# A hybrid retention and attention block on one core: `w_do` behind the first q,k gemm, both side products behind `w_o`, splits one gemm ahead, and a new order of the tail

## The chip, the cores and the metric

The kernel runs on one core of one Trainium2 chip. The metric is the time on the device in microseconds; the median of three runs of the kernel before is 1240.94 us (1239.77 to 1241.05).

## The reference

One layer on x of shape (1, 512, 1024), all in float32:

```python
u = rmsnorm(h, g_pre_mix)
proj = u @ w_in         # retention q,k,v,gate | dilated q,k,v | gates gr, ga
yr = rmsnorm(retention(rq, rk, rv, positions)) * silu(rg)      # 4 heads
ya_branch = yr @ w_ret_out
ya = dilated_attention(aq, ak, av, positions)   # 3 groups, merged by softmax denominators
yb_branch = ya @ w_dil_out
mixed = sigmoid(gr + b0) * ya_branch + sigmoid(ga + b1) * yb_branch
h = h + rmsnorm(mixed @ w_o, g_post_mix)
f = square(relu(rmsnorm(h, g_pre_mlp) @ w_up)) @ w_down
h = h + rmsnorm(f, g_post_mlp)
gate = sigmoid(rmsnorm(h, g_pre_ple) @ w_ple_gate + b_ple_gate)
h = h + rmsnorm(gate * (p @ w_ple_in), g_post_ple)
```

## The kernel before, in words

Every float32 product is made of three matmuls. `split` writes a float32 value as a rounded high part (ACT copies and rounds) and a low part (DVE subtracts); `PASSES` multiplies high with high, high with low and low with high. A gemm of 512 columns and 1024 rows of weights is 4 groups of 24 matmuls of 128x512, each in a PSUM bank; one of 512 rows is 4 groups of 12.

The order of the work is written out by hand. SP's queue carries the weight loads in one chain (`load`): a ring of raw 512 KB units, in the order of the list `loads`. `prep_next` splits the next unit of `plan` into a weight tile and tops up the ring; a gemm calls it while its last group runs. `later(lag, f)` puts off a piece by so many steps of PE, counted by `pump` after each group of three matmuls; `flush` runs all that is put off, and `drain` the steps of the attention that `filler` strews through gemms. What the text leaves free a scheduler decides: it orders each engine's queue, and pieces in `tc.high_priority()` come earlier.

The stages, with the names that the change touches:

1. `u`, transposed, then per dilated group g three gemms (v, q, k). `row_tables` makes the row of 1/rms (`rrow`) with four transposes on PE. The attention of a group runs inside the next gemms; `stream_order` moves its maxima and denominators between the two orders of tokens with small DMAs on ACT's and POOL's queues.
2. Four gate gemms; `gate_evac` applies the sigmoid and stores to DRAM (`zd`). Ahead of the fourth, `merge` combines the three groups: DVE scales them, 32 transposes on PE turn them round, and the result `y` goes to DRAM (`yd`). `left_sums` makes the sums of `u` for the 7-product scheme of `quartet`.
3. Four retention heads (`head`): a q,k gemm, rotation by `rope_pair`, then `quartet` with seven quarter products of two weight units each ("11", 1, "12", 2, 4, 7, "22"), scores, the retained products, and `flip`, which transposes the head's result and stores it (`yrd`).
4. `w_do`: two gemms of 48 on `yT` fetched from DRAM, times the fetched gate; `w_ro`: per head two gemms of 48 on `yrT`, fetched and split (`halved`) at the start of the head. `mix_out` joins both.
5. `w_o`: the first half with k outermost, then four token blocks; `wo_second` ends each block with its norm, and `residual_features` puts off the block's eight transposes (`to_features`) by a lag of 8. Then `e_first`, the first half of p @ w_ple_in, 24 matmuls, and `w_up`.
6. `w_up` and `w_down` by quartets, then the last two units of `w_down` by token block, again with `residual_features` and lag 8; the second half of p @ w_ple_in; then `w_ple_gate`, the first half by blocks, then the second, where `gated` makes sigmoid times e and `finish` the norm, the update and the two stores of a block. The last block is cut in two pieces of 256 columns.

The lag, for example, is given here:

```python
def residual_features(t, base, r, gain, rs, dst, rows, lag):
    ...
        later(lag, lambda v=v, n=n: to_features(dst, v, t, 4 * n))
```

## Time and profile before

| | |
|---|---|
| median of three runs | 1240.94 us |
| the profiled execution, its own time | 1239.94 us |
| its span | 1238.1 us |
| mean granted clock of PE in it | 0.996 |
| PE busy | 1213.0 us (98%), 5636 matmuls |
| DVE busy | 803.7 us (65%) |
| ACT busy | 593.1 us (48%) |
| POOL busy | 54.4 us (4%) |

The table is read from the first part of the profile's page. PE is busy nearly all the time, so what an edit can move lies in the stretches where PE waits, and in those where its granted clock is below full speed. The waits say for whom PE waited, the windows show how much of a stretch it was busy and how full the other engines were in it, and the timeline shows the single wait in its place. Weight loads into PE (PEld) overlap the matmuls. Ends of matmuls are modelled, so a row's length runs a little past the start of the next row.

### The profile page before, as it was taken

To read this page: it belongs to the slowest core of one execution; us is meant where nothing else is said; L and a number is where in the kernel's file an instruction comes from. 1 tells how busy PE (TensorE), PEld (TensorE's weight loads), DVE (VectorE), ACT (ScalarE), POOL (GpSimd) and SP (SyncE) were. 2 spreads that over 40 slices of the span, in tenths; PEclk is the share of its full clock that TensorE was granted. 3 is DMA by queue.
4 is the path that set the end of the run, shared out by engine and by line. 5 is a ranking of instruction groups with operands and counts; after the bars stand their busy time and mean duration, and the time that the engine had idled before them with its cause. 6 is when DMAs were issued, how large, how long until landed. Compare 5 with 4: busy or idle time off the path is not lost.

```text
span 1238.1 us, 15113 instructions
## 1 busy us (share of the span) xinstructions
PE 1213.0 (98%) x5636; PEld 990.2 (80%) x5636; DVE 803.7 (65%) x1215; ACT 593.1 (48%) x991; POOL 54.4 (4%) x100
## 2 busy tenths in 40 slices
...
GB/s 340 129 118 69 61 94 89 76 204 76 128 61 229 85 119 114 142 102 119 150 120 261 115 170 102 305 119 182 57 153 66 88 187 52 97 209 140 103 48 69
DMA packets 54617, 159.39 MB, mean 129 GB/s; under 512 B 8720, under 2 KB 8976, under 8 KB 54544
## 3 DMA queue, kind: packets, MB, share of 16 engines
...
q14 instruction: 29, 0.24, 0.1%
...
## 4 chain that ended last, share of the span: by engine, by line
PE 92%; DVE 3%; DMA 2%; ACT 2%; issue 1%; POOL 0%; DVEq 0%; POOLq 0%; ACTq 0%
PE a L233 50%; PE b L686 14%; PE a L999 11%; PE a L686 7%; PE b L464 2%; PE b L768 2%; PE b L494 2%; PE b L482 1%; DVE t L69 1%; ACT s L66 1%; PE b L753 1%; DMA t<-in_xT_dram 1%; DMA t<-in_x_dram 1%; DVE t L283 1%; PE b L306 1%
## 5 line engine op out<-in xcount | busy, mean ns | idle before, releaser
L69 DVE TENSOR_TENSOR w<-t,w 128x1024 fp32r<-128x1024 f32 (+1 forms) x248 | 296.1, 1204 | 158.2 <-ACT w L66 156.0
L66 ACT ACTIVATE w<-t 128x1024 fp32r<-128x1024 f32 (+1 forms) x248 | 257.5, 1045 | 280.0 <-PE a L233 100.8
L233 PE MATMUL a<-u,w 128*128 128x512 f32 x1536 | 376.5, 398 | 3.3 <-ACT u L66 2.4
L233 PEld LDWEIGHTS a<-u,w 128*128 128x128 f32 x1536 | 283.2, 189 | 66.8 <-issue 4.0
L69 DVE TENSOR_TENSOR t<-t,t 128x1024 f32<-128x1024 f32 (+4 forms) x193 | 194.4, 1031 | 23.5 <-ACT t L66 18.3
L686 PE MATMUL b<-w,t 128*128 128x512 f32 x696 | 162.5, 389 | 0.0
L686 PEld LDWEIGHTS b<-w,t 128*128 128x128 f32 x696 | 130.6, 188 | 27.1
L999 PE MATMUL a<-u,w 128*128 128x512 f32 x576 | 134.0, 389 | 0.0
L999 PEld LDWEIGHTS a<-u,w 128*128 128x128 f32 x576 | 108.1, 188 | 22.4
L233 PE MATMUL a<-w,u 128*128 128x512 f32 (+1 forms) x504 | 118.0, 390 | 5.1 <-ACT w L66 5.1
L233 PE MATMUL a<-t,w 128*128 128x512 f32 x480 | 110.5, 391 | 1.0 <-ACT t L66 0.6
L233 PEld LDWEIGHTS a<-w,u 128*128 128x128 f32 x504 | 91.7, 192 | 23.4 <-ACT w L66 5.1
L233 PEld LDWEIGHTS a<-t,w 128*128 128x128 f32 x480 | 89.8, 188 | 20.6 <-ACT t L66 1.3
L233 PE MATMUL a<-w,t 128*128 128x512 f32 x432 | 100.5, 391 | 0.0
L233 PEld LDWEIGHTS a<-w,t 128*128 128x128 f32 x432 | 80.6, 188 | 16.5
L69 DVE TENSOR_TENSOR t<-a,t 128x512 f32<-128x512 f32 x72 | 55.6, 773 | 58.2 <-ACT t L66 30.2
L66 ACT ACTIVATE s<-b 128x512 f32<-128x512 f32 (+1 forms) x74 | 44.6, 609 | 94.4 <-PE b L482 40.5
L468 DVE CUSTOM_DVE_ANT_0 s<-b,masks 128x128 f32<-128x128 f32 (+1 forms) x96 | 27.2, 321 | 84.7 <-PE b L464 84.7
L66 ACT ACTIVATE t<-t 128x512 fp32r<-128x512 f32 (+1 forms) x61 | 45.5, 770 | 38.3 <-DVE t L69 36.6
L66 ACT ACTIVATE s<-s,st 128x128 f32<-128x128 f32 (+1 forms) x96 | 40.0, 418 | 25.4 <-DVE st L471 25.3
L69 DVE TENSOR_TENSOR s<-a,t 128x512 f32<-128x512 f32 x40 | 26.4, 687 | 38.7 <-PE a L233 31.4
L66 ACT ACTIVATE t<-s 128x256 f32<-128x256 f32 (+3 forms) x90 | 39.1, 481 | 23.3 <-DVE s L69 19.7
...
## 6 DMA issues: line engine op xcount, KB each, us to landing
t<-in_w_in_dram SPq DMA_DIRECT2D x104, 512.0 KB
t<-in_w_down_dram SPq DMA_DIRECT2D x38, 512.0 KB
t<-in_w_up_dram SPq DMA_DIRECT2D x32, 512.0 KB
t<-in_w_ret_out_dram SPq DMA_DIRECT2D x16, 512.0 KB
t<-in_x_dram SPq DMA_DIRECT2D x8, 512.0 KB
...
```

Source lines behind the costliest of these rows:

```text
L66: nc.scalar.activation(o, i, f, **kw)
L69: nc.vector.tensor_tensor(o, x, y, op=op)
L233: nc.tensor.matmul(ps, l, r, start=(k == 0 and q == 0), stop=(k == n - 1 and q == 2))
L283: return nc.vector.scalar_tensor_tensor(o, x, s, y, op0=op0, op1=op1)
L306: nc.tensor.transpose(b[:, f * P:(f + 1) * P], src[:, f * P:(f + 1) * P], ident)
L464: nc.tensor.matmul(sb[hh][:, q * w:(q + 1) * w], at(qT, p0 + q)[rows, t * P:(t + 1) * P], at(kT, p0 + q)[rows, k0:k0 + w], start=True, sto ...
L468: nc.vector.tensor_tensor_reduce(out=sm[:, i, :], in0=sb[hh][:, q * w:(q + 1) * w], in1=mk, scale=1.0, scalar=NEG, op0=OP.add, op1=OP.max, ...
L482: nc.tensor.transpose(tb[:, c * P:(c + 1) * P], sm[:, i, j * P:(j + 1) * P], ident)
L494: nc.tensor.matmul(pv[:, s * HD:(s + 1) * HD], got["t"][:, c * P:(c + 1) * P], at(v, t - nb + 1 + j)[:, s * HD:(s + 1) * HD], start=(j == ...
L686: nc.tensor.matmul(ps[t], f(k, i, t), w[:, j, k2], start=(first and k == 0 and n == 0), stop=(k == 3 and n == 2), skip_group_check=not first)
L768: nc.tensor.matmul(b, sc[j][:, i1, c:c + P], vh[j][:, i2, :], start=(n == 0), stop=(n == last))
L999: nc.tensor.matmul(state["ps"][t], w[:, i, k2, t * P:(t + 1) * P], vT[:, x, k], start=(k == 0 and n == 0), stop=(k == 7 and n == 2))
```

## The change

- The gate columns come in the order 21 to 24; the first two gate gemms store to DRAM (`z0d`), the last two keep their result on chip (`z1`).
- The maxima and denominators of group 0 are put in stream order as soon as group 1 is started, and the eight scatters of `merge` that were on POOL's queue go to SP's.
- `merge` puts off its four turns (eight transposes each) by lags of 32 to 44, and splits each result at once into `yT`; `yd` goes.
- `w_do` and its weight units move from behind the last head to behind the q,k gemm of head 0, with `left_sums`; its product with `z1` goes to DRAM (`ybd`).
- `row_tables` is put off by 4 steps.
- In `w_ro` the operands of the next head are split between the two gemms of a head; `ybd` and `z0d` are fetched on POOL's queue.
- Both halves of p @ w_ple_in run behind `w_o`, both go to DRAM and are fetched on POOL's queue; the lags are 16 and 14 behind `w_o` and 12 behind `w_down`, and the `flush` ahead of `w_ple_gate` goes.
- In the tail the multiply with `g_post_ple` moves from `finish` to `gated`, and the updates of block 2 are issued behind the last block's first operations.

The diff, cut to its core:

```diff
-    for c in (23, 24, 21, 22):
+    for c in (21, 22, 23, 24):
         add_units(w_in, c)
     for h in range(H):
         add_units(w_in, 3 * h)
+        if not h:
+            for n in range(2):
+                add_units(w_do, n)
         add_quartet(lambda kh, nh, k, h=h: w_in[3 * h + 2 - nh, 2 * kh + k], EARLY)
-    for n in range(2):
-        add_units(w_do, n)
     for h in range(H):
         for n in range(2):
             add_units(w_ro[h], n)
     for n in range(2):
         add_units(a["w_o"], n)
-    add_units(a["w_ple_in"], 0)
+    for n in range(2):
+        add_units(a["w_ple_in"], n)
...
+        if g == 1:
+            stream_order(lambda c: sc[0][:, c], lambda t: M[0][:, t])
+            stream_order(lambda c: sc[1][:, c], lambda t: DEN[0][:, t])
...
-                eng = nc.gpsimd if c % 2 else nc.scalar
+                eng = nc.sync if c % 2 else nc.scalar
...
         def scaled(o, nt_, al):
...
-        for p in range(4):
+        def turn(p):
             b = bank()
             for c in range(4):
                 nc.tensor.transpose(b[:, c * P:(c + 1) * P], at(N[1], c)[:, p * P:(p + 1) * P], ident)
...
             for t in range(NT):
                 nc.tensor.transpose(b[:, t * P:(t + 1) * P], at(N[0], t)[:, p * P:(p + 1) * P], ident)
             tt(y, b, y, OP.add)
-            nc.scalar.dma_start(yd[p], y)
+            yh = big((P, 2, 512), F32R)
+            split(yh[:, 0], yh[:, 1], y)
+            yT.append(yh)
+
+        for p in range(4):
+            later(32 + 4 * p, lambda p=p: turn(p))
 
...
+        if not h:
+            flush()
+            left_sums()
+            for n in range(2):
+                gemm(2, list_feed(yT), do_out(n, z1[n]), wstat=True)
...
-    def gate_evac(n, k):
+    z0d = [pdr.tile([P, 512], F32, name=f"z0d{i}") for i in range(KT)]
+    ybd = [pdr.tile([P, 512], F32, name=f"ybd{i}") for i in range(KT)]
+
+    def gate_evac(n, k, keep=None):
         def f(t, ps):
-            z = half()
             i = 4 * n + t
-            tt(z, ps, rrow, OP.mult)
+            z = half() if keep is None else at(keep, t)
+            with tc.high_priority():
+                tt(z, ps, rrow, OP.mult)
             act(z, z, AF.Sigmoid, bias=cols[:, 1 + k, i:i + 1])
-            nc.scalar.dma_start(zd[k][i], z)
+            if keep is None:
+                nc.scalar.dma_start(z0d[i], z)
         return f
 
-    for n in range(4):
-        if n == 3:
+    def do_out(n, z):
+        def f(t, ps):
+            x = at(z, t)
+            tt(x, ps, x, OP.mult)
+            nc.scalar.dma_start(ybd[4 * n + t], x)
+        return f
+
+    for n in range(2):
+        gemm(4, uT, gate_evac(n, 0), wstat=True)
+    z1 = [pair_tiles() for _ in range(2)]
+    for n in range(2):
+        if n:
             drain()
             merge()
-            left_sums()
-        gemm(4, uT, gate_evac(n % 2, 1 - n // 2), wstat=True)
-
...
-    xs = fetch(yd)
-    yb = fetch(zd[1])
-    yT = halved(xs)
     xs = fetch(yrd[0])
-    for n in range(2):
-        gemm(2, list_feed(yT), do_out(n), wstat=True)
     yacc = [big((P, 2, 512)) for _ in range(4)]
+    yrT = halved(xs)
     for h in range(H):
-        yrT = halved(xs)
         if h + 1 < H:
             xs = fetch(yrd[h + 1])
         else:
-            z0 = fetch(zd[0])
-        for n in range(2):
-            gemm(2, list_feed(yrT), half_out(yacc, n, h == 0) if h + 1 < H else mix_out(n), wstat=True)
+            yb, z0 = ([at(x, i) for i in range(KT)] for x in (fetch(ybd, nc.gpsimd.dma_start), fetch(z0d, nc.gpsimd.dma_start)))
+        gemm(2, list_feed(yrT), half_out(yacc, 0, h == 0) if h + 1 < H else mix_out(0), wstat=True)
+        nxt = halved(xs) if h + 1 < H else None
+        gemm(2, list_feed(yrT), half_out(yacc, 1, h == 0) if h + 1 < H else mix_out(1), wstat=True)
+        yrT = nxt
 
...
-        residual_features(t, h1[t], r, g_pre, rs1[:, t:t + 1], vT, (r0[t], z), 8)
+        residual_features(t, h1[t], r, g_pre, rs1[:, t:t + 1], vT, (r0[t], z), 16 if t < 3 else 14)
         nc.gpsimd.dma_start(h1d[t], h1[t])
 
     gemm(4, mix, wo_second)
 
-    def e_first(t, ps):
-        x = half()
-        act(x, ps)
-        nc.scalar.dma_start(ed[t], x)
-
-    gemm(1, list_feed(pT), e_first)
+    def e_out(n):
+        def f(t, ps):
+            x = half()
+            act(x, ps)
+            nc.scalar.dma_start(ed[n][t], x)
+        return f
+
+    for n in range(2):
+        gemm(1, list_feed(pT), e_out(n))
     flush()
 
...
-        residual_features(t, h1[t], r, g_pre2, rs2[:, t:t + 1], hT, [part(t, n) for n in range(2)], 8)
-
-    pT = side()
-    e = {0: pair_tiles(), 1: pair_tiles()}
-    for t in range(NT):
-        nc.gpsimd.dma_start(at(e[0], t), ed[t])
-    gemm(1, list_feed(pT), lambda t, ps: act(at(e[1], t), ps))
-    flush()
+        residual_features(t, h1[t], r, g_pre2, rs2[:, t:t + 1], hT, [part(t, n) for n in range(2)], 12)
+
+    e = {n: pair_tiles() for n in range(2)}
+    for n in range(2):
+        for t in range(NT):
+            nc.gpsimd.dma_start(at(e[n], t), ed[n][t])
 
...
-        stt(z, ps, rs2[:, t:t + 1], b_ple[:, sl], OP.mult, OP.add)
+        i = stt(z, ps, rs2[:, t:t + 1], b_ple[:, sl], OP.mult, OP.add)
         act(z, z, AF.Sigmoid)
         x = at(e[n], t)[:, c]
-        tt(x, x, z, OP.mult)
-        parts.setdefault(t, []).append(sumsq(x))
-
-    def finish(t):
+        j = nc.vector.tensor_tensor(z, x, z, op=OP.mult)
+        parts.setdefault(t, []).append(sumsq(z))
+        tt(x, z, g_post3[:, sl], OP.mult)
+        return i.ins, j.ins
+
+    def finish(t, behind=None):
         r = rstd(parts[t], D)
         for n, sl in enumerate(halves):
-            tt(at(e[n], t), at(e[n], t), g_post3[:, sl], OP.mult)
-        for n, sl in enumerate(halves):
-            stt(h1[t][:, sl], at(e[n], t), r, h1[t][:, sl], OP.mult, OP.add)
+            with ExitStack() as st:
+                if behind:
+                    st.enter_context(tc.issue_after(behind[n]))
+                stt(h1[t][:, sl], at(e[n], t), r, h1[t][:, sl], OP.mult, OP.add)
             (nc.scalar if n else nc.sync).dma_start(out[t * P:(t + 1) * P, sl], h1[t][:, sl])
 
...
-                gated(t, 1, cs, ps[:, :w])
-        finish(t)
+                ins = gated(t, 1, cs, ps[:, :w])
+        if t != NT - 2:
+            if t == NT - 1:
+                finish(t - 1, ins)
+            finish(t)
```

Three places show how instructions move. Names are those of the tiles (w a weight tile, a and b banks of PSUM, t and s tiles in SBUF); `a<-w,t` is a matmul or an operation that writes a.

PE between `w_o` and `w_up`: in the kernel before, the end of the transposes of block 1, the side product (banks a_6723 to a_6753), the transposes of block 3 and the first matmuls of `w_up` (a_6788).

```order
L306 MATMUL b_6687<-ident,s_6621 128x128 x4
L233 MATMUL a_6723<-w_6434,t_6285 128x512 x3
L233 MATMUL a_6723<-w_6434,t_6288 128x512 x3
L233 MATMUL a_6733<-w_6434,t_6285 128x512 x3
L233 MATMUL a_6733<-w_6434,t_6288 128x512 x3
L233 MATMUL a_6743<-w_6434,t_6285 128x512 x3
L233 MATMUL a_6743<-w_6434,t_6288 128x512 x3
L233 MATMUL a_6753<-w_6434,t_6285 128x512 x3
L233 MATMUL a_6753<-w_6434,t_6288 128x512 x3
L306 MATMUL b_6765<-ident,s_6706 128x128 x4
L306 MATMUL b_6772<-ident,s_6709 128x128 x4
L233 MATMUL a_6788<-u_6444,w_6642 128x512 x6
```

In the changed kernel, from the end of the first side product:

```order
L234 MATMUL a_6725<-w_6420,t_6267 128x512 x3
L234 MATMUL a_6725<-w_6420,t_6270 128x512 x3
L307 MATMUL b_6737<-ident,s_6590 128x128 x4
L307 MATMUL b_6744<-ident,s_6593 128x128 x4
L307 MATMUL b_6781<-ident,s_6678 128x128 x4
L307 MATMUL b_6788<-ident,s_6681 128x128 x4
L234 MATMUL a_6754<-w_6614,t_6267 128x512 x3
L234 MATMUL a_6754<-w_6614,t_6270 128x512 x3
L234 MATMUL a_6764<-w_6614,t_6267 128x512 x3
L234 MATMUL a_6764<-w_6614,t_6270 128x512 x3
```

The transposes of blocks 2 and 3 stand together ahead of the second side product, whose banks begin with a_6754; `w_up` follows that product.

DVE at the start of head 0, where it prepares the second quarter's two weight units: in the kernel before w_3251 and w_3263, made between sums of weights and products of the rotation.

```order
L69 TENSOR_TENSOR t_3204<-s_3195,t_3204 128x512
L69 TENSOR_TENSOR w_3239<-t_3111,w_3239 128x1024
L69 TENSOR_TENSOR t_3111<-t_3111,t_3133 128x1024
L69 TENSOR_TENSOR w_3251<-t_3100,w_3251 128x1024
L69 TENSOR_TENSOR s_3280<-a_3232,t_673 128x512
L69 TENSOR_TENSOR w_3263<-t_3111,w_3263 128x1024
L69 TENSOR_TENSOR w_3274<-t_3242,w_3274 128x1024
```

In the changed kernel w_3409 is the second unit of that quarter; ahead of it stand products of `w_do` (banks a_3371 to a_3401) and sums of `left_sums` (t_3245, t_3249 and the low parts t_3256, t_3258).

```order
L69 TENSOR_TENSOR t_2637<-a_3371,t_2637 128x512
L69 TENSOR_TENSOR t_3258<-t_3245,t_3257 128x512
L69 TENSOR_TENSOR t_3256<-t_3249,t_3255 128x512
L69 TENSOR_TENSOR t_2638<-a_3386,t_2638 128x512
L69 TENSOR_TENSOR t_3249<-t_3249 128x2x256
L69 TENSOR_TENSOR t_3197<-t_3197,t_3219 128x1024
L69 TENSOR_TENSOR t_2638<-a_3401,t_2638 128x512
L69 TENSOR_TENSOR t_3258<-t_3249,t_3257 128x512
L69 TENSOR_TENSOR w_3409<-t_3197,w_3409 128x1024
```

The unit is made behind all of `w_do`'s products with z1, while before nothing of `w_do` or `left_sums` stood there.

DVE at the end of the program: before, block 2's updates (t_8946) ahead of the last piece's evacuation (s_9652), and the multiply with g_post_ple (t_9324) between the last sum and the norm.

```order
L283 SCALAR_TENSOR_TENSOR t_8946<-t_9264,st_9587,t_8946 128x512
L283 SCALAR_TENSOR_TENSOR t_8946<-t_9266,st_9587,t_8946 128x512
L283 SCALAR_TENSOR_TENSOR s_9652<-a_9627,rs_8943,t_9322 128x256
L69 TENSOR_TENSOR t_9266<-t_9266,s_9652 128x256
L69 TENSOR_TENSOR st_9659<-st_9460,st_9624 128x1
L69 TENSOR_TENSOR st_9661<-st_9659,st_9656 128x1
L69 TENSOR_TENSOR t_9266<-t_9266,t_9324 128x512
L292 TENSOR_SCALAR st_9663<-st_9661 128x1
L283 SCALAR_TENSOR_TENSOR t_8947<-t_9264,st_9665,t_8947 128x512
L283 SCALAR_TENSOR_TENSOR t_8947<-t_9266,st_9665,t_8947 128x512
```

In the changed kernel, from the last piece's evacuation (s_9634) on; block 2 is t_8977, block 3 t_8978:

```order
L284 SCALAR_TENSOR_TENSOR s_9634<-a_9609,rs_8974,t_9284 128x256
L1084 TENSOR_TENSOR s_9634<-t_9275,s_9634 128x256
L69 TENSOR_TENSOR t_9275<-s_9634,t_9286 128x256
L69 TENSOR_TENSOR st_9642<-st_9411,st_9572 128x1
L293 TENSOR_SCALAR st_9644<-st_9642 128x1
L69 TENSOR_TENSOR st_9652<-st_9453,st_9605 128x1
L284 SCALAR_TENSOR_TENSOR t_8977<-t_9273,st_9646,t_8977 128x512
L284 SCALAR_TENSOR_TENSOR t_8977<-t_9275,st_9646,t_8977 128x512
L69 TENSOR_TENSOR st_9654<-st_9652,st_9638 128x1
L293 TENSOR_SCALAR st_9656<-st_9654 128x1
L284 SCALAR_TENSOR_TENSOR t_8978<-t_9273,st_9658,t_8978 128x512
L284 SCALAR_TENSOR_TENSOR t_8978<-t_9275,st_9658,t_8978 128x512
```

Block 2's norm and updates now stand behind the last piece's products and ahead of the last sum of block 3 (st_9654); the multiply stands with the products.

## Rows read from the trace of the kernel before

**Rows 1.** The page: its head with the span, part 1 with busy time of each engine, its share of the span and the number of instructions, and part 4, the shares of the chain that ended last, by engine.

```profile
span 1238.1 us, 15113 instructions
...
PE 1213.0 (98%) x5636; PEld 990.2 (80%) x5636; DVE 803.7 (65%) x1215; ACT 593.1 (48%) x991; POOL 54.4 (4%) x100
...
PE 92%; DVE 3%; DMA 2%; ACT 2%; issue 1%; POOL 0%; DVEq 0%; POOLq 0%; ACTq 0%
```

**Rows 2.** Waits of PE over the whole span: the operation that waited, what it waited for after the arrow, then us in total, times, and the longest in us.

```profile
PE a L233 <- ACT w L66: 5.1, 1, 5.1
...
PE b L371 <- POOL rs L294: 1.7, 2, 1.3
...
PE b L482 <- ACT s L66: 0.6, 1, 0.6
```

**Rows 3.** Windows: the stretch in us from the span's start, its length, then the busy time and the number of instructions of PE, PEld, DVE, ACT and POOL, the mean granted clock of PE as a share of full speed, the busy share of the DMA engines and GB/s.

```profile
345.00:384.00 39.00, 37.39 (x188) 30.29 (x186) 29.36 (x55) 26.92 (x44) 4.28 (x8) 1.00 0.36 123
...
816.00:840.00 24.00, 20.36 (x102) 16.45 (x100) 20.74 (x40) 16.05 (x34) 6.19 (x10) 0.99 0.52 189
...
840.00:885.00 45.00, 45.00 (x193) 36.96 (x193) 11.09 (x11) 18.09 (x31) 0.00 (x0) 0.97 0.31 106
...
1160.00:1194.00 34.00, 32.35 (x159) 26.51 (x158) 31.55 (x62) 22.18 (x46) 5.32 (x10) 1.00 0.19 62
...
1194.00:1215.00 21.00, 21.00 (x94) 17.41 (x93) 12.55 (x18) 9.89 (x19) 0.00 (x0) 1.00 0.00 1
...
1215.00:1238.00 23.00, 13.46 (x83) 11.93 (x81) 13.14 (x29) 4.56 (x12) 2.51 (x4) 0.87 0.24 92
```

**Rows 4.** The chain that ended last, in order of time, in head 0: start, length, engine, tile, line and count of one run of 128x512 matmuls.

```profile
424.36 5.44 PE b L686 x24
```

**Rows 5.** PE's timeline from the last tiles of `w_o` to `w_up`: start, length, engine, line, operation, output and inputs, shape of the stationary operand and of the moving one, count, and in brackets the idle time before it and what ended it.

```profile
828.17 1.03 PE L306 MATMUL b<-ident,s 128*128 128x128 f32 x8
...
835.88 1.23 PE L306 MATMUL b<-ident,s 128*128 128x128 f32 x8 [1.22 <-DVE s L69]
...
839.52 10.64 PE L233 MATMUL a<-u,w 128*128 128x512 f32 x38 [2.42 <-ACT u L66]
```

**Rows 6.** PE's timeline in the fourth gate gemm and the start of the first q,k gemm: first and last row of the stretch. The 32 transposes of `merge` lie between them, one to six in a row, with 89 matmuls in all.

```profile
359.69 5.15 PE L233 MATMUL a<-u,w 128*128 128x512 f32 x22
...
383.93 2.35 PE L233 MATMUL a<-u,w 128*128 128x512 f32 x9 [0.87 <-DVE s L69]
```

**Rows 7.** DVE's timeline in `merge` and in head 0: three products of a 128x512 piece, and three pieces of 128x1024, one behind the other.

```profile
360.92 1.90 DVE L69 TENSOR_TENSOR t<-t,m 128x512 f32<-128x512 f32 x3
...
415.89 3.49 DVE L69 TENSOR_TENSOR w<-t,w 128x1024 fp32r<-128x1024 f32 x3
```

**Rows 8.** PE's timeline at the start of `w_do` and in `w_ro` of head 0.

```profile
671.28 0.96 PE L233 MATMUL a<-t,w 128*128 128x512 f32 x3 [0.31 <-ACT t L66]
...
672.43 0.33 PE L785 MATMUL b<-ident,s 128*128 128x128 f32 x1 [0.19 <-DVE s L283]
...
716.73 0.96 PE L233 MATMUL a<-t,w 128*128 128x512 f32 x3 [0.31 <-ACT t L66]
...
718.08 1.20 PE L233 MATMUL a<-t,w 128*128 128x512 f32 x4 [0.38 <-DVE t L69]
```

**Rows 9.** Timelines of POOL's and SP's queues from `merge` on: start, the time from the first issue to the end of the last, queue, line, what is moved, count.

```profile
361.08 4.28 POOL L559 DMA_DIRECT2D mg<-mg  x8 [152.66 <-DVE m L69]
...
365.79 11.57 SPq L82 DMA_DIRECT2D t<-in_w_in_dram  x4
```

**Rows 10.** DMA issues by line: what is moved, queue, count, KB each, and the median time in us from issue to landing.

```profile
t<-h1d POOLq DMA_DIRECT2D x4, 512.0 KB, 4.1
```

**Rows 11.** Groups of ACT's instructions: line, operation, output and inputs, count, busy time in us and mean ns of one, and the idle time before them with what ended it.

```profile
L66 ACT ACTIVATE w<-t 128x1024 fp32r<-128x1024 f32 (+1 forms) x248 | 257.5, 1045 | 280.0 <-PE a L233 100.8 <-PE b L686 63.0 <-PE a L999 51.1
...
L66 ACT ACT_TABLE_LOAD x23 | 29.5, 1283 | 4.8 <-DMA t<-t 2.8 <-PEq L1152 1.2 <-ACT s L66 0.4
```

**Rows 12.** ACT's timeline in the gate gemms: a table load and the exponential behind it.

```profile
279.01 1.28 ACT L66 ACT_TABLE_LOAD   x1
280.30 0.40 ACT L66 ACTIVATE s<-s,st 128x128 f32<-128x128 f32 x1
```

**Rows 13.** PE's timeline at the end of `w_down` and in the first tiles of `w_ple_gate`: the transposes that waited.

```profile
1163.79 0.66 PE L306 MATMUL b<-ident,s 128*128 128x128 f32 x4 [1.05 <-DVE s L69]
...
1191.00 0.63 PE L306 MATMUL b<-ident,s 128*128 128x128 f32 x4 [0.60 <-DVE s L69]
```

**Rows 14.** Timeline of all engines from 1214: PE's last run of 128x512 matmuls, the updates of token block 2, the last evacuation, the multiply with g_post3, the power and the last store.

```profile
1213.71 14.75 PE L233 MATMUL a<-w,u 128*128 128x512 f32 x87
...
1228.22 1.41 DVE L283 SCALAR_TENSOR_TENSOR t<-t,st,t 128x512 f32<-128x512 f32 x2
...
1229.55 0.48 DVE L283 SCALAR_TENSOR_TENSOR s<-a,rs,t 128x256 f32<-128x256 f32 x1
...
1231.59 0.69 DVE L69 TENSOR_TENSOR t<-t,t 128x512 f32<-128x512 f32 x1
...
1232.48 0.55 POOL L294 TENSOR_TENSOR st<-st,mhalf 128x1 f32<-128x1 f32 x1 [4.30 <-DVE st L292]
...
1234.51 0.34 ACTq L1074 DMA_DIRECT2D out_dram<-t  x1
```

56 lines of the change are left out of this document (25 added, 31 removed).

## The prediction

> **What bounds the kernel now.** I read the page first: PE is busy in 98% of the span, and the chain that ended last is PE for 92% [rows 1]. The change removes no matmul, so all it can win is time in which PE stands still or runs slowly. Then the waits of PE in total [rows 2], the windows around the edited stages [rows 3], and PE's timeline at each wait. Of PE's 25 idle us, 5.1 lie at the start [rows 2] and 9.5 in the last window [rows 3]; the change reaches the rest. As units: 24 matmuls of 128x512 take 5.44 us [rows 4], 0.227 each; eight 128x128 transposes about 0.9 [rows 5].
>
> **Part by part.**
>
> *Row tables by lag.* Their four transposes wait 1.7 us for POOL [rows 2]. The text defers them, but in the order of the changed kernel they stand at the same place, ahead of the first rotary gemm. Worth nothing.
>
> *Merge.* Now the 32 transposes stand singly among the matmuls of the fourth gate gemm, and PE waits several times: 1.61 are lacking in the window [rows 3], the longest wait is 0.87 [rows 6]. From 359.69 to 386.28 pass 26.6 us for 89 matmuls (20.2) and 32 transposes (3.5): with the switching 2.7 are lost [rows 6]. In the new order four blocks of eight stand 12 matmuls (2.7 us) apart, the first behind the whole fourth gate gemm. Their inputs are scaled under that gemm's 21.8 us, where 16 products and sums take 9.6 at 0.60 each (three in a row 1.90, one 0.69, and likewise 1.13 for the double size, three in 3.49) [rows 7]; a block asks one ACT copy, one sum, and a split that only w_do needs. I take 2.5 back (1.5 to 2.7).
>
> *Start of w_do and of w_ro.* The waits at 671.28 and 672.43 (0.31, 0.19), and at 716.73 and 718.08 (0.31, 0.38) [rows 8], are for splits of yT, the last head's flips and splits of yrT. Both splits now come a gemm or more ahead (10.9 us for w_ro), and the flips stand in fours inside w_ro. Gain 0.5 and 0.7. The four stores and four loads of yT go; no other wait hung on them.
>
> *w_do behind the first q,k gemm.* 96 matmuls move, 21.8 us, with left_sums under them. The eight products go to DRAM on ACT's queue and are read some 300 us later. On DVE the stretch is close. The fifth group of w_do is there 13.6 us after its start; from its product on, DVE has 19 pieces at 0.60 and four at 1.13 [rows 7] to do up to the second weight unit of head 0's second quarter (w_3409 in the order shown): 13.6 + 0.3 + 11.4 + 4.5 = 29.8. PE wants it after 96 + 24 + 12 matmuls: 29.9. Nothing to spare, so I charge 0.4 (0 to 2).
>
> *SP's queue.* Eight scatters of a0n leave POOL, where eight take 4.28 us behind DVE's scaled weights at 361 [rows 9], 7 us into the fourth gate gemm (its first 24 matmuls, 5.4, precede 359.69 [rows 6]), for SP, ahead of w_do's loads. Before, the loads behind it went out at 365.79 [rows 9], 12 us into that gemm; by DVE's order I count the same 12 for w_do's. With 4.1 for landing, the longest time to land of a 512 KB transfer that the trace gives [rows 10], and 1.0 for ACT's half of the split [rows 11] the first unit is ready at 17; DVE's half stands behind that gemm's last product, at 22. Cost nothing, 5 us of cover; what it costs without is a rival below. The 16 fetches of yb and z0 go from SP to POOL's queue, which is busy 4% [rows 1], a whole w_ro head ahead: nothing.
>
> *Sigmoids.* The change has 25 activation-table loads for 23, 1.28 us each [rows 11]. In the gate gemms PE waits for ACT but once, 0.6 [rows 2], so two more (2.6 us on ACT) are worth 0; bounds -2.6 and, should the new order lose even that wait, +0.6. The row shows the next activation at 280.30, 1.29 after the load began at 279.01 [rows 12], nothing between. The Trainium skill (ScalarE: Activation LUTs, "What ACT_TABLE_LOAD costs") adds a drain of about 1.38 us to each switch; the trace shows none here, and by that rule the lower bound would be -5.3.
>
> *w_o to w_up.* w_o ends at 828.17; the transposes of block 3 wait till 835.88, w_up till 839.52 [rows 5]. In these 11.35 us PE has 24 matmuls and 16 transposes, 7.2; 4.2 are lost. Then 38 matmuls take 10.64 us, not 8.6: another 2.0, and the granted clock of that window is 0.97 against 1.00 around it [rows 3], so some 2.7 us at 1.2 GHz, after 3.6 us of idling in 12. After: transposes of block 1, e0 (5.44), blocks 2 and 3, e1 (5.44), w_up. Block 3 is ready 7.7 us after w_o as now, and 7.2 of work precede it: 0.5 of waiting, and up to 0.9 for banks that ACT and DVE must empty. w_up was ready 3.6 us after block 3's transposes began; with e1 between, 6.3 pass, and that wait goes. Lost 1.4 instead of 6.2: gain 4.8 (3.3 to 5.7). The second side product itself only comes from the other place.
>
> *w_down to w_ple.* Waits of 1.05 and 0.60 [rows 13] and some switching, about 2.0 in all, go if the lags fit. The 24 matmuls that covered there are gone, and the last blocks' transposes stand inside w_ple. Counted along DVE's new order, block 2, the next weight unit and block 3 are ready 0.1 to 0.4 us before PE wants them. I take 1.5 (0 to 2.3).
>
> *Tail.* The multiply with g_post3, 0.69 at 1231.59 [rows 14], leaves the last chain, and block 2's pair of updates (1.41 at 1228.22), which held the last evacuation till 1229.55, moves behind it. But in DVE's new order that pair now stands between the last products and the last sum. The last matmul ends at 1228.46; evacuation 1228.6, both products till 1230.4, block 2's sum, POOL's power (0.55) and the pair till 1232.7, then the last sum, power and pair: the last store at about 1235.0 against 1234.51. Loss 0.5 (0.8 of loss to 0.3 of gain).
>
> Sum: 2.5 + 0.5 + 0.7 - 0.4 + 4.8 + 1.5 - 0.5 = 9.1. The profiled execution took 1239.94, which gives 1230.8; it stands 1.0 under the median of the runs, 1240.94, so against that median the forecast is **1231.8**. All good ends together give a gain of 12.8, 1228.1; all bad ends 0.6.
>
> **Rivals.** A measurement of this kernel tells about 0.2%, 2.5 us, from no change: the boundaries are 1238.5 and 1243.4.
>
> *DVE becomes the bound at w_ple.* Between 1160 and 1194 DVE is busy 31.55 of 34 us [rows 3]. Without 5.44 of PE's work 28.6 are left, 27.1 by my term: if all of DVE's work must happen there it takes 31.6, 4.5 more: 1236.3. Against it: in the window behind, DVE has 12.55 of 21 [rows 3], and block 3's part can run under w_ple. Chance 0.17.
>
> *Head 0 waits for its weights.* If DVE's 16 us up to that unit run 15% longer, PE stands 2.4 us, and behind a wait of 2.42 the clock fell, for 2.0 [rows 5]: 1231.8 + 4.4 = 1236.2. Against it: from 1160 to 1194 DVE was as full, and PE's waits were 1.05 and 0.60 [rows 3, 13]. Chance 0.10.
>
> *The slow clock stays.* If the short waits left between w_o and w_up bring the clock down too, 2.0 come back: 1233.8. Against it: waits of 1.05 and 0.60 between 1160 and 1194 left it at 1.00 [rows 3, 13]. For it stands the Trainium skill (TensorE: Matmul & The Clock Gate, "A second HAM failure mode: psum-queue depth-cycling"), by which frequent small pauses between groups cost the clock. Chance 0.10.
>
> *Most waits only move.* All that is removed waits for DVE or ACT; if those chains follow the matmuls to their new places, only the clock's 2.0 is won: 1238.9. Chance 0.06.
>
> *Slower: SP's queue stops.* SP works in order, and behind the scatters stand w_do's units, a decay table, head 0's units and the four loads for left_sums; DVE in turn has the first unit's split ahead of the merge's sums. If the scaled weights come more than 5 us later than counted (the last exponentials stand at the end of an ACT queue with more table loads), each further us is one in which PE stands. A lateness of one gate gemm, 21.8, costs 16.8, and 2.0 for the clock: 1231.8 + 18.8 = 1250.6. It ends slower by over 0.2% from 14.6 us of lateness on. Against it: the same weights came 7 us into the gemm before [rows 9], and two table loads are 2.6 us. Chance 0.06.
>
> **How the numbers follow.** The forecast itself has 0.51. Faster by over 0.2%: the forecast 0.48, w_ple 0.14, head 0 0.08, the clock 0.10: 0.80. Within: what is left of these, most of the waits that move, a mild queue: 0.13. Slower: the queue and a little of the rest, 0.07. The range runs from all good ends together, 1228.1, to 1238.5, which takes in the three dearer cases on the fast side.
>
> **What would show it.** Right: no wait of PE over 0.5 us from the fourth gate gemm to head 0; w_up starts 14 to 16 us after w_o's last matmul with the clock at 1.00; w_ple's start loses under 0.7; the last store goes out 6.5 us after the last matmul. Wrong: PE waiting for a weight unit in head 0's first quarters, for a load behind SP's scatters, or for DVE inside w_ple; a granted clock under 1.00 between w_o and w_up.

## The result and the profile after

The changed kernel takes 1230.37 us in the median of six runs (1229.78 to 1231.44); the kernel before, run beside it, takes 1240.99 (six runs). The ratio is 0.9916, with an interval from 0.9904 to 0.9929: 0.8% faster, 10.6 us. The forecast was 1231.8 (1228.1 to 1238.5), faster with a chance of 0.80. The profiled execution took 1230.01, with a span of 1228.2 and a mean clock of 0.997.

First the page of the changed kernel, its first and fourth part, against [rows 1]:

```profile
span 1228.2 us, 15112 instructions
...
PE 1209.0 (98%) x5636; PEld 989.6 (81%) x5636; DVE 804.2 (65%) x1214; ACT 595.5 (48%) x991; POOL 62.0 (5%) x112
...
PE 96%; DVE 2%; issue 1%; ACT 0%; POOL 0%; DMA 0%; DVEq 0%; POOLq 0%; ACTq 0%
```

The matmuls are the same 5636. PE's share of the chain rose from 92% to 96%: what went is standing still. All waits of PE over the whole span, against [rows 2] (operation, what it waited for, us in total, times, longest):

```profile
PE a L234 <- ACT w L66: 5.4, 1, 5.4
PE b L372 <- POOL rs L295: 0.8, 1, 0.8
PE b L307 <- DVE s L69: 0.6, 2, 0.3
PE b L484 <- ACT s L66: 0.6, 1, 0.6
PE b L307 <- DVE u L69: 0.5, 1, 0.5
```

Only five kinds are left, and the first two stand in the first 35 us, which the change hardly reaches. The windows around the edited stages, against [rows 3] (stretch, length, busy time and count of PE, PEld, DVE, ACT and POOL, granted clock, DMA share, GB/s):

```profile
345.00:380.00 35.00, 35.00 (x173) 29.37 (x173) 26.32 (x43) 22.81 (x28) 0.00 (x0) 1.00 0.39 139
816.00:845.00 29.00, 28.20 (x134) 22.52 (x133) 19.00 (x33) 18.23 (x35) 4.28 (x6) 1.00 0.52 188
845.00:885.00 40.00, 40.00 (x178) 33.15 (x177) 15.00 (x13) 20.04 (x32) 0.00 (x0) 1.00 0.31 115
1150.00:1184.00 34.00, 33.66 (x163) 27.56 (x161) 30.06 (x61) 18.92 (x42) 6.10 (x9) 1.00 0.22 81
1204.00:1228.00 24.00, 12.88 (x80) 11.46 (x78) 13.29 (x27) 4.57 (x12) 1.91 (x4) 0.83 0.23 88
```

Through the fourth gate gemm PE is busy without a gap. Between `w_o` and `w_up`, and at the start of `w_ple_gate`, it stands for 0.80 and 0.34 us. No window ahead of the tail has a clock under 1.00. What stands where `w_o` waited for `w_up` [rows 5], PE's timeline:

```profile
821.12 1.03 PE L307 MATMUL b<-ident,s 128*128 128x128 f32 x8
821.91 5.70 PE L234 MATMUL a<-w,t 128*128 128x512 f32 x24
827.45 1.03 PE L307 MATMUL b<-ident,s 128*128 128x128 f32 x8
828.79 0.63 PE L307 MATMUL b<-ident,s 128*128 128x128 f32 x4 [0.31 <-DVE s L69]
829.91 0.66 PE L307 MATMUL b<-ident,s 128*128 128x128 f32 x4 [0.49 <-DVE u L69]
830.47 5.73 PE L234 MATMUL a<-w,t 128*128 128x512 f32 x24
836.17 16.21 PE L234 MATMUL a<-u,w 128*128 128x512 f32 x69
```

Both side products run at full speed (24 in 5.7), and `w_up` begins 15.05 us after `w_o` ended at 821.12, with 48 matmuls and 24 transposes in between, where before 11.35 passed for 24 matmuls and 16 transposes.

To place the whole difference, the starts of the matmuls in the two traces were compared, stage by stage: for each matmul, how much later than usual the next one starts, added up. The usual spacing is the median for the matmul's shape over the traces of all fourteen kernels (0.227 us for 128x512); the first row has the time to the first matmul too. In us:

| stretch of the program | before | changed | gain | forecast |
|---|---|---|---|---|
| start, to 60 | 9.60 | 9.30 | 0.30 | 0 |
| gate gemms, 280 to 360 | 7.12 | 6.02 | 1.10 | 0 |
| merge, 360 to 400 | 2.75 | 0.03 | 2.72 | 2.5 |
| `w_do` moved, head 0, 400 to 480 | 0.07 | -0.02 | 0.09 | -0.4 |
| start of `w_do`, `w_ro`, 660 to 720 | 2.38 | 0.28 | 2.10 | 1.2 |
| `w_o` to `w_up`, 820 to 860 | 6.02 | 1.93 | 4.09 | 4.8 |
| `w_down` to `w_ple_gate`, 1160 to 1200 | 2.26 | 0.92 | 1.34 | 1.5 |
| last matmul's start to the end of the span | 9.96 | 11.62 | -1.66 | -0.5 |

That makes 10.1 of the 9.9 by which the spans differ; the rest of the program is 0.2 longer.

The start can't be read finer than this: in the kernels below that leave the start alone, one profiled execution each, the 120th matmul starts between 35.4 and 37.7 us, mostly because the wait for the row tables (0.8 to 2.2) varies. So each experiment is read by the stretch that it edits, and by the **middle**, from the start of the matmul behind the 120th to the last one's start: 1191.78 before, 1180.49 in the changed kernel.

### The profile page after: what moved, and what is told of

Same layout as the page of the kernel before. It is cut to its first block, busy times and chain, and to the rows that moved or that the text cites. A ratio compares the mean times of both kernels' runs of the same rounds, so it can differ in the third digit from the quotient of the medians.

```text
span 1228.2 us, 15112 instructions
## 1 busy us (share of the span) xinstructions
PE 1209.0 (98%) x5636; PEld 989.6 (81%) x5636; DVE 804.2 (65%) x1214; ACT 595.5 (48%) x991; POOL 62.0 (5%) x112
## 4 chain that ended last, share of the span: by engine, by line
PE 96%; DVE 2%; issue 1%; ACT 0%; POOL 0%; DMA 0%; DVEq 0%; POOLq 0%; ACTq 0%
PE a L234 53%; PE b L696 15%; PE a L1020 11%; PE a L696 7%; PE b L466 2%; PE b L783 2%; PE b L496 2%; PE b L484 1%; PE b L768 1%; PE b L804 1%; DVE t L284 0%; DVE t L69 0%; PE b L307 0%; ACT s L66 0%; POOL st L295 0%
## 5 line engine op out<-in xcount | busy, mean ns | idle before, releaser
L69 DVE TENSOR_TENSOR t<-t,t 128x1024 f32<-128x1024 f32 (+4 forms) x179 | 184.9, 1057 | 21.0 <-ACT t L66 18.6
L66 ACT ACTIVATE t<-t 128x512 fp32r<-128x512 f32 (+1 forms) x55 | 42.2, 788 | 38.1 <-DVE t L69 38.0
L66 ACT ACTIVATE t<-s 128x256 f32<-128x256 f32 (+3 forms) x94 | 41.7, 488 | 23.9 <-DVE s L69 20.3
L66 ACT ACTIVATE s<-a 128x512 f32<-128x512 f32 x56 | 32.7, 593 | 38.5 <-PE a L234 30.5
```

What stands on the lines that cost most here:

```text
L66: nc.scalar.activation(o, i, f, **kw)
L69: nc.vector.tensor_tensor(o, x, y, op=op)
```

## The experiments

Each was timed in rounds beside the kernel before; a ratio is to that kernel. The edits are to the changed kernel.

### The tail: the old order, and an earlier update

The old text of `gated` and `finish` back, all else as changed:

```diff
-        tt(x, z, g_post3[:, sl], OP.mult)     # in gated
...
+            tt(at(e[n], t), at(e[n], t), g_post3[:, sl], OP.mult)     # in finish
...
-        if t != NT - 2:
-            if t == NT - 1:
-                finish(t - 1, ins)
-            finish(t)
+        finish(t)
```

> The changed kernel with the order of the tail of the kernel before (multiply with g_post_ple in finish, block 2 finished at once); all else as changed. My theory, that the new tail lost time on DVE: the changed kernel's last store is issued 7.0 us after its last matmul (1223.6 against 1216.6) where before it was 6.3, so this kernel should show 6.3 again, and a time 0.7 shorter than the changed kernel's 1230.4, about 1229.7. From the last store to the end of the span the changed kernel has 4.6, the one before 3.6. If that 1.0 belongs to the order too (block 2's second store goes out on ACT's queue 1.4 us ahead of block 3's, so both land together), the time is 1228.7. Rival: DVE's order in the tail costs nothing, and the 1.7 between the two tails is the landing of the last store as it falls by chance: no difference, 1230.4, with the end 4.6 behind the last store.

Measured: 1230.03, 0.9908 (0.9892 to 0.9924), which the runs don't tell from the changed kernel. In the trace the last matmul starts 10.95 before the end instead of 11.62. The second kernel keeps the new products, but takes block 2's power early, issues its first update behind the first piece's multiply and its second one behind the last evacuation, with both stores on SP:

```diff
+                if t == NT - 2:
+                    r2 = rstd(parts[t], D)
...
+            update(t - 1, 0, r2, first[2])
+            update(t - 1, 1, r2, ins[0], nc.sync)
+            with tc.high_priority():
+                finish(t)
```

> The changed kernel with another tail: the norm of block 2 is taken as soon as its sums are there, its two updates stand in DVE's queue one ahead of the last evacuation and one right behind it, and both its stores go out on SP's queue. My theory, that block 2's norm and pair between the last products and the last sum are what holds the end: counted with the rows of the changed kernel, the last chain is evacuation at 0.3 behind the last matmul, sigmoid 0.8, product 1.3, square 1.7, sum 2.3, power 2.6 to 3.1, first update 3.2, second 3.8, last store 4.6 instead of 7.0: 2.4 us less, and 3.4 less if the landing goes back to 3.6 as well. 1227.0 to 1228.0. Rival: the end is set by the landing of the stores, and an earlier issue only waits longer: 1229.5 to 1230.4.

Measured: 1228.70, 0.9898 (0.9880 to 0.9917); the interval overlaps the changed kernel's, and in the trace the last matmul starts 9.57 before the end. The chain behind the last matmul, in the changed kernel (timeline of DVE, POOL and ACT's queue):

```profile
1216.91 0.48 DVE L284 SCALAR_TENSOR_TENSOR s<-a,rs,t 128x256 f32<-128x256 f32 x1 [1.02 <-PE a L234]
...
1218.68 0.15 DVE L69 TENSOR_TENSOR st<-st,st 128x1 f32<-128x1 f32 x1
...
1219.17 0.55 POOL L295 TENSOR_TENSOR st<-st,mhalf 128x1 f32<-128x1 f32 x1 [9.38 <-DVE st L69]
1219.75 1.41 DVE L284 SCALAR_TENSOR_TENSOR t<-t,st,t 128x512 f32<-128x512 f32 x2 [0.66 <-POOL st L295]
...
1221.08 0.15 DVE L69 TENSOR_TENSOR st<-st,st 128x1 f32<-128x1 f32 x1
...
1221.57 0.55 POOL L295 TENSOR_TENSOR st<-st,mhalf 128x1 f32<-128x1 f32 x1 [1.85 <-DVE st L293]
1222.15 1.41 DVE L284 SCALAR_TENSOR_TENSOR t<-t,st,t 128x512 f32<-128x512 f32 x2 [0.73 <-POOL st L295]
```

and in the one with the early update:

```profile
1215.76 0.74 DVE L284 SCALAR_TENSOR_TENSOR t<-t,st,t 128x512 f32<-128x512 f32 x1
...
1216.68 0.48 DVE L284 SCALAR_TENSOR_TENSOR s<-a,rs,t 128x256 f32<-128x256 f32 x1 [0.17 <-PE a L234]
1217.08 0.74 DVE L284 SCALAR_TENSOR_TENSOR t<-t,st,t 128x512 f32<-128x512 f32 x1
1218.53 0.42 DVE L69 TENSOR_TENSOR st<-st,st 128x1 f32<-128x1 f32 x2
1219.28 0.55 POOL L295 TENSOR_TENSOR st<-st,mhalf 128x1 f32<-128x1 f32 x1 [4.05 <-DVE st L293]
1219.87 1.41 DVE L284 SCALAR_TENSOR_TENSOR t<-t,st,t 128x512 f32<-128x512 f32 x2 [0.73 <-POOL st L295]
```

From the last evacuation to the last pair pass 5.24 us in the first and 3.19 in the second: block 2's power and pair stood in front of block 3's sum, as the prediction read from the order. The last store goes out 7.0 us behind the last matmul's start in the changed kernel, 6.3 in the old order (as before), 4.95 with the early update.

But the old order gives back only 0.7 of the 1.7 that the tail lost. There the last store is as early as before, and the span still ends 4.62 us behind it instead of 3.63. One us has another cause.

### The end of POOL's queue

Behind its last power, POOL has an instruction at the end of the program, a DRAIN, that the views leave out; it is in the trace's records. Counted from the end of that power, it takes the longer, the more DMAs were issued on POOL's queue, and the span ends 0.8 behind it (1.1 in the kernel with 60):

| kernel | DMAs on POOL's queue | its length, us |
|---|---|---|
| before | 52 | 4.34 |
| second side product moved back | 60 | 4.99 |
| changed | 64 | 5.31 |

That is 0.081 per DMA, counted by number and not by size: the kernel before has eight scatters of 1 KB among its 52, and lies on the same line as kernels with fetches of 256 KB in their place. The change added 16 fetches of `yb` and `z0` and four of `e`, and took eight scatters away. Fetches on SP again:

```diff
-            yb, z0 = (... fetch(ybd, nc.gpsimd.dma_start), fetch(z0d, nc.gpsimd.dma_start))
+            yb, z0 = (... fetch(ybd), fetch(z0d))
```

> The changed kernel with the 16 fetches of yb and z0 on SP's queue, where the kernel before had its fetches, not on POOL's. The runs so far show that the span ends 0.8 behind the end of POOL's last drain, and that this drain ends 4.34 us behind the last power in the kernel before, which has 52 DMAs on POOL's queue, 4.99 in the kernel with one side product between w_down and w_ple, which has 60, and 5.31 in the changed kernel and the other two experiments, which have 64: 0.081 us for each DMA. My theory: the drain at the end costs POOL so much for each DMA that its queue ever carried. With 48 it takes 4.0, so the end comes 1.3 earlier: about 1229.1 against 1230.4. SP's own end, 1.65 us before POOL's in the changed kernel, is then still the earlier one. Rival: the end waits for the stores to land, and POOL's drain only stretches till then; then nothing changes in the 5.3. Second rival, against the whole edit: SP's queue, on which the fetches stand ahead of w_o's last units, delays weights, and w_o or w_up waits: over 1231.

Measured: 48 DMAs, 4.02 us, as the two kernels with 52 and 64 foretold; the tail is 10.30 instead of 11.62, the middle unchanged (1180.65). The median, 1229.55 (0.9907, 0.9893 to 0.9921), is only 0.8 under the changed kernel's, and the intervals overlap. The profile shows the 1.3; the timing doesn't resolve it.

### The second side product back behind `w_down`

```diff
-    for n in range(2):
-        gemm(1, list_feed(pT), e_out(n))
+    gemm(1, list_feed(pT), e_out(0))
     flush()
...
-        residual_features(..., [part(t, n) for n in range(2)], 12)
+        residual_features(..., [part(t, n) for n in range(2)], 8)
+    pT = side()
...
+    gemm(1, list_feed(pT), lambda t, ps: act(at(e[1], t), ps))
+    flush()
```

> The changed kernel with the second side product (24 matmuls) back between w_down and w_ple, with the lag of 8 and the flush there; behind w_o only the first one, lags of 16 and 14 kept. My theory: behind w_o the 24 matmuls cover the chain from block 3's transposes to w_up. Without them w_up waits some 2.7 us (3.6 from the start of the transposes, 0.9 of which is the transposes), and the granted clock falls for some 2.0 more; the 1.05 and 0.60 of waiting before w_ple come back for the 0.97 that the changed kernel loses there: 1230.4 + 2.7 + 2.0 + 1.3 = 1236.4. Rival: it is the longer lags, which put the transposes of blocks 2 and 3 behind the first side product, that took the waits away: w_up then waits under 1.0, the clock stays, and the time is about 1232. On the clock: if it falls only behind waits of more than 2 us, the window behind w_up's start shows about 0.97 here; if it also falls for short ones it would have fallen in the changed kernel, where it is 1.00.

Measured: 1237.28, 0.9964 (0.9950 to 0.9978). PE's timeline at the place where the changed kernel has its second product, and the window:

```profile
828.62 0.63 PE L307 MATMUL b<-ident,s 128*128 128x128 f32 x4 [0.31 <-DVE s L69]
829.74 0.66 PE L307 MATMUL b<-ident,s 128*128 128x128 f32 x4 [0.49 <-DVE u L69]
834.55 17.69 PE L234 MATMUL a<-u,w 128*128 128x512 f32 x64 [4.16 <-ACT u L66]
```

```profile
816.00:842.00 26.00, 21.05 (x91) 16.63 (x90) 17.51 (x32) 13.65 (x27) 4.28 (x6) 0.87 0.69 238
```

The transposes stand at the same time as in the changed kernel, with the same two short waits. `w_up` then waits 4.16, and the clock of the window falls to 0.87. The loss of that stretch is 8.53 against 1.93, and 6.02 in the kernel before. So the longer lags win nothing without this product in its new place. Whether the product wins as much with the lag of 8 was not run.

### The turns of merge at once

```diff
-            later(32 + 4 * p, lambda p=p: turn(p))
+            turn(p)
```

> The changed kernel with the four turns of merge called at once, ahead of the fourth gate gemm in the text, not put off by lags of 32 to 44; yT still stays on the chip, w_do still stands behind the first q,k gemm. My theory: the lags alone took away the losses of merge, which were 2.7 us by the rows before; PE again has the transposes one by one among the fourth gate gemm's matmuls, behind DVE's scaling and ACT's copies, and the time is 1232.9 to 1233.1. Rival: the waits came from the way over the DRAM (the stores on ACT's queue between the copies) or from DVE's work on left_sums in the same stretch, which is moved away here too: at most 1.0 of loss, 1231.0.

Measured: 1233.03, 0.9928 (0.9913 to 0.9944), where the theory pointed. But the trace puts only 1.3 of the 2.7 into the merge (1.35 lost there against 0.03); most of the rest is the start, where this execution waits 2.1 for the row tables and the changed kernel's 0.8. So the number was met in part by luck. The window:

```profile
345.00:385.00 40.00, 39.39 (x198) 32.53 (x197) 29.33 (x51) 27.07 (x38) 0.00 (x0) 1.00 0.42 148
```

So taking the lags out loses 1.3. The kernel with `w_do` back behind the last head, below, is the other half of this trial: there the lags stay, and `left_sums` and the way of `y` over DRAM are back in this stretch. It loses 0.5. The kernel before, which has neither the lags nor the lighter load (nor group 0's maxima in stream order ahead of `merge`), loses 2.7. So 1.3 hangs on the lags and 0.5 on the load; the other 0.9 is lost only without both, or belongs to the smaller edits, which no run tells apart.

### DVE made dearer under head 0

Each product of `w_do` computed twice:

```diff
+            tt(half(), ps, x, OP.mult)
             tt(x, ps, x, OP.mult)
```

> The changed kernel in which each of the eight products of w_do with z1 is made twice on DVE (once into a scratch tile that nothing reads); 0.60 us each, 4 of them, 2.4 us, behind w_do's fifth group. It tells how close head 0 is to waiting for DVE. In the changed kernel the weight unit w_3409 is ready 30.2 us after w_do's start and wanted at 29.9 to 30.2. My theory: there is no slack, so all 2.4 us come out as waiting of PE in head 0's second quarter, where it can move only one matmul ahead; with the clock 2.0 more if it falls: 1232.8, or 1234.8. Rival: the scheduler, or the pieces of left_sums that are wanted later, make room, and the time stays within 0.5 of 1230.4.

Measured: 1230.35, 0.9915 (0.9902 to 0.9929): nothing. My theory, by which the delay reaches PE, fell. PE's timeline around the second quarter of head 0 shows why:

```profile
421.09 2.88 PE L696 MATMUL a<-w,u 128*128 128x512 f32 x12
423.81 3.80 PE L768 MATMUL b<-t,t 128*128 128x512 f32 x23
427.58 3.01 PE L696 MATMUL a<-w,u 128*128 128x512 f32 x12
```

The scheduler put 23 of the head's scores (L768) ahead of the weights that were late. In the changed kernel they come behind. The experiment changed the order along with the load, so it doesn't tell what a delay in the same order would cost.

### Holding the waiting transposes behind matmuls

Row tables and block 3's transposes were issued behind the last matmul so far, so that PE would have work in place of the waits of 0.8 to 2.2 and of 0.31 and 0.49. Block 3's lag becomes 12, and its `to_features` is held back in the same way:

```diff
+    def held_back(f):
+        with tc.issue_after(mm[0]):     # the last matmul written so far
+            f()
...
-            later(4, tables)
+            later(4, lambda: held_back(tables))
...
-        residual_features(t, h1[t], r, g_pre, rs1[:, t:t + 1], vT, (r0[t], z), 16 if t < 3 else 14)
+        residual_features(t, h1[t], r, g_pre, rs1[:, t:t + 1], vT, (r0[t], z), 16 if t < 3 else 12)
```

> The changed kernel with two groups of transposes held back on PE behind matmuls: those of the row tables behind the 12th matmul of the first rotary gemm, where the text of the change wanted them but the scheduler did not put them, and those of token block 3 behind the 12th matmul of the second side product, not ahead of its first. My theory, from the waits left in the changed kernel: the row tables wait 0.8 to 2.1 us for POOL there, and between w_o and w_up 2.0 us are lost, 0.31 and 0.49 of them in waits of the transposes for DVE; 2.7 us later both inputs are ready. w_up then starts 3.6 us behind the transposes' start with 0.9 + 2.7 of work between: just ready. Gain 1.0 to 1.7 at the tables and 1.0 to 2.0 behind w_o: 1227.5 +- 0.7. Rival: the transposes are held up by banks that DVE and ACT have to empty, or the rotation then waits for the tables, and the waits only move: 1230 or more.

Measured: 1231.20, 0.9920 (0.9906 to 0.9933): no gain. PE's timeline at the start and behind `w_o`:

```profile
31.65 4.33 PE L240 MATMUL a<-u,w 128*128 128x512 f32 x12 [2.52 <-ACT t L66]
...
832.80 3.06 PE L240 MATMUL a<-w,t 128*128 128x512 f32 x12 [1.98 <-ACT s L66]
```

The waits moved to the banks: the matmuls that should cover need a bank which ACT has still to empty. Behind `w_o` ACT splits a weight and makes two sums first. At the start its copies out of the banks stand behind sums over x, and the chain goes back to the load of x, which lands at 29.6. Behind the wait of 2.52 there the clock fell too: the granted clock from 31 to 36 is 0.70, and the 12 matmuls behind the wait take 4.33 instead of about 3. A second kernel combines this with the early update of the tail and the fetches on SP:

> The changed kernel with the early norm of block 2 in the tail, the fetches of yb and z0 on SP's queue, and the two groups of transposes held back: three edits in different places. My theory: they add up, 1.7 (measured for the tail), 1.3 and 2.5 to 3: 1224.5 to 1225.5. Rival: the last one that ends the span is hidden behind another: with POOL's drain shorter, the landing of the last store sets the end, and of the 3.0 for tail and drain together only some 2.4 are to be had: 1226.

Measured: 1227.96, 0.9895 (0.9881 to 0.9908). The tail is 8.26, as the two edits to it promise; the held transposes give nothing, since `w_o` to `w_up` loses 3.9 instead of 1.9. The same wait stands in it:

```profile
831.50 4.32 PE L240 MATMUL a<-w,t 128*128 128x512 f32 x12 [1.98 <-ACT s L66]
```

Behind an equal wait, 12 matmuls took 3.06 in the one kernel and 4.32 in the other, where the window's clock is 0.93 instead of 1.00.

### `w_do` back behind the last head

The products over DRAM as before, `left_sums` ahead of the fourth gate gemm, the lags of merge kept:

```diff
-        if not h:
-            flush()
-            left_sums()
-            for n in range(2):
-                gemm(2, list_feed(yT), do_out(n, z1[n]), wstat=True)
...
             merge()
+            left_sums()
...
+    for n in range(2):
+        gemm(2, list_feed(yT), do_out(n), wstat=True)
```

> The changed kernel with w_do back behind the last head: merge's results and the sigmoids z1 go over DRAM again, left_sums stands ahead of the fourth gate gemm again; the turns of merge stay put off, and all the rest (w_ro's splits, side products, tail) is as changed. My theory: moving w_do won little by itself, only the waits at its start (0.31 + 0.19 and the switching, 0.5 to 1.1), and it cost nothing because left_sums fits under it; the gain at merge comes from the turns put off. So 1231.0 to 1231.5. Rival: merge's gain needs left_sums out of its way; with 16 sums and 16 splits of it on DVE and ACT in the fourth gate gemm again, PE waits in the first q,k gemm or in head 0's first quarter: 1232.5 or more. Second rival: a w_do without products to hide behind frees head 0, and the time is 1230 or less.

Measured: 1230.52, 0.9924 (0.9912 to 0.9936). The two waits at its start are back:

```profile
669.28 0.96 PE L233 MATMUL a<-t,w 128*128 128x512 f32 x3 [0.31 <-ACT t L66]
670.43 0.33 PE L796 MATMUL b<-ident,s 128*128 128x128 f32 x1 [0.18 <-DVE s L283]
```

With what stands around them that stretch loses 1.1 instead of 0.3, and the merge 0.5 instead of nothing. The middle is 1181.52 against 1180.49: the whole move is worth 1.0. Its eight fewer fetches on POOL shorten the end by 0.65, so the time hardly shows it: it falls between the theory and the second rival.

### The operands of `w_ro` split at the head's start

```diff
-    yrT = halved(xs)
     for h in range(H):
+        yrT = halved(xs)
...
-        nxt = halved(xs) if h + 1 < H else None
...
-        yrT = nxt
```

> The changed kernel with the operands of w_ro split at the start of each head again, not between the two gemms of the head before. My theory: at the first switch of heads PE waits again 0.31 for ACT and 0.38 for DVE, as in the kernel before at 716.7 and 718.1, and the losses between 700 and 720 are 1.3 us again where the changed kernel has 0.1: 1231.2 to 1231.6. At the later heads nothing is lost, as nothing was before. Rival: the wait came from the fetch of yrd behind w_do's on SP's queue, and with w_do gone from there it is not there: 1230.4.

Measured: 1232.22, 0.9937 (0.9925 to 0.9949). PE's timeline:

```profile
709.80 2.20 PE L234 MATMUL a<-t,w 128*128 128x512 f32 x9
712.31 0.97 PE L234 MATMUL a<-t,w 128*128 128x512 f32 x3 [0.31 <-ACT t L66]
713.65 2.59 PE L234 MATMUL a<-t,w 128*128 128x512 f32 x10 [0.38 <-DVE t L69]
```

The waits of [rows 8] are back to the hundredth. But 12 matmuls, 2.72 us at 0.227, take 3.85 here from 709.80 to 713.65: 1.13 lost for 0.69 of waiting. By the spacing of starts the stretch loses 1.3 more than in the changed kernel. With the 0.8 that `w_do`'s old place costs at its start, that is all of the 2.1 in the table.

### The best pieces together, and the gates without priority

The early update of the tail with the fetches on SP, without the held transposes:

> The changed kernel with the two edits that won by themselves: block 2's norm and updates early in the tail, and the fetches of yb and z0 on SP's queue (48 DMAs on POOL's). My theory: POOL's last power ends 3.5 us behind the last matmul, as in the kernel with the early norm alone, its drain 4.02 later, the span 0.77 behind that: 8.3 behind the last matmul where the changed kernel has 11.6; 3.3 less, so 1227.1. SP's own end (7.1 behind the last matmul there) is just ahead of POOL's. Rival: the two gains overlap, since the landing of the last store takes the place of the drain: 1228.0 or more.

Measured: 1228.58, 0.9905 (0.9892 to 0.9918). The tail is 8.26, 3.4 shorter than in the changed kernel (3.3 worked out); the middle (1180.16) isn't longer. The time is 1.8 under the changed kernel's, and the intervals of the two overlap: better in the trace, not told apart by the runs.

Last, the evacuation of the gates without its high priority, which changes ACT's order and its table loads:

```diff
-            with tc.high_priority():
-                tt(z, ps, rrow, OP.mult)
+            tt(z, ps, rrow, OP.mult)
```

> The changed kernel without the high priority of the gate gemms' product with the row table; the scheduler's order then has 19 activation-table loads, not 25, so ACT saves 7.7 us in the stretch of the gate gemms, and the evacuations on DVE come later. My theory: table loads cost nothing there, since PE does not wait for ACT in the gate gemms in the changed kernel; what counts for PE is how often its order switches between transposes, scores and gate matmuls, some 0.1 us each: within 0.7 of 1230.4, either way. Rival, by ACT: the loads delay the exponentials and with them PE; without six of them the losses between 280 and 340, 5.7 us, shrink by 2 or more: 1228.5. Rival, by the banks: without priority the evacuation comes late and PE waits for banks: 1232 or more.

Measured: 1230.84, 0.9930 (0.9918 to 0.9942). The groups of table loads, in this kernel and in the changed one:

```profile
L66 ACT ACT_TABLE_LOAD x19 | 24.4, 1283 | 4.7 <-DMA t<-t 2.8 <-PEq L1176 1.2 <-ACT s L66 0.4
```

```profile
L66 ACT ACT_TABLE_LOAD x25 | 32.1, 1283 | 5.9 <-DMA t<-t 2.8 <-ACT s L66 1.6 <-PEq L1177 1.2
```

Six loads and 7.7 us of ACT less made nothing faster, and PE waits for ACT nowhere in that stretch in either kernel. That agrees with the loads being hidden; the order changed along with them, so this run alone doesn't show it. The gate gemms lose 7.01 instead of 6.02: nearly all of the 1.1 that they gained unforeseen goes with the order that the priority makes. PE is busy for the whole of that stretch in all three kernels, so no wait explains it. The starts of the matmuls tell where it lies: PE changes directly between 128x128 transposes (L484) and the attention's 64x128 score matmuls (L466) 35 times in the kernel before, 27 times in the changed one and 36 times here, and 4.1, 3.2 and 4.2 us are lost at these changes, about 0.12 each. That is 0.9 of the 1.1, and agrees with the theory above, which put such changes at some 0.1 each. Why such a change costs that much, no run shows.

## Why the prediction was right, step by step

**What bounds the kernel:** right. The gain is PE's standing time. The sum misses a tenth of the span's change, 9.1 against 9.9.

**Row tables:** right; their wait is still there. Its size lies between 0.8 and 2.2 in the kernels that leave it alone, which the prediction didn't know.

**Merge:** right in size (2.7 for 2.5). The lags were only part of the reason: with them alone taken out the merge loses 1.3, with `left_sums` and the way over DRAM alone put back 0.5, and the kernel before, without either, 2.7. The prediction gave all of it to the new order.

**Start of `w_do` and `w_ro`:** the direction and the place were right, the term was too small, 1.2 for 2.1. It added the waits as the rows give them, and the two in `w_ro` cost 1.13 for 0.69 in the experiment; a row's idle time begins at the modelled end of a matmul, so it is no full account. The next term has the same fault.

**`w_o` to `w_up`:** 4.1 for 4.8. `w_up` started after 15.05 (forecast 14 to 16), block 3's transposes 7.67 after `w_o` (forecast 7.7). What is left was put at 1.4 and is 1.93, though the rows show only 0.80 of waiting. The 4.16 that the single product leaves shows the mechanism, with its clock.

**SP's queue:** right within 0.6 us. In the changed kernel the scatters and the loads behind them stand in SP's timeline so:

```profile
360.38 4.99 SPq L564 DMA_DIRECT2D mg<-mg  x8
365.47 1.96 SPq L82 DMA_DIRECT2D t<-in_w_dil_out_dram  x4
```

`w_do`'s first load goes out 12.6 us into the fourth gate gemm (12 counted), and nothing waited for it.

**Head 0:** no loss where 0.4 was charged. `w_do` begins at 399.95. DVE makes its part of w_3409 in the first of these two pieces, till 430.2, 30.2 us later (29.8 counted):

```profile
428.97 2.36 DVE L69 TENSOR_TENSOR w<-t,w 128x1024 fp32r<-128x1024 f32 x2 [0.30 <-ACT w L66]
```

and PE, in the same stretch:

```profile
430.37 0.39 PE L768 MATMUL b<-t,t 128*128 128x512 f32 x1
430.59 1.75 PE L696 MATMUL a<-w,t 128*128 128x512 f32 x7
```

In front of the first matmul that needs DVE's part stand, in the order of PE, two that need only ACT's part, the last of the 14 in the row ahead (427.19 to 430.37), and one of the scores; it starts at 430.59. The prediction had PE there at 29.9 us and overlooked these three, 0.7 us. In the doubled products the scheduler put 23 scores there.

**`w_down` to `w_ple_gate`:** 1.3 for 1.5. What is still lost there is 0.9, where the prediction's sign was under 0.7, and one wait is left:

```profile
1174.40 1.23 PE L307 MATMUL b<-ident,s 128*128 128x128 f32 x8 [0.34 <-DVE s L69]
```

The rival by which DVE becomes the bound is refuted: DVE is busy 30.06 of 34 us in that window, and PE 33.66.

**Tail:** the step that failed in size, -1.7 for -0.5. The order of DVE costs 0.7, where 0.5 was worked out: the last store goes out 6.7 us behind the end of the last matmul, not 6.5. The other 1.0 is POOL's end, which hangs on the number of its DMAs. The prediction costed the fetches on POOL's queue at nothing because the queue is busy 4%; the early update and the fetches on SP show both parts separately.

**Sigmoids:** loads cost nothing, as forecast: PE waits for ACT nowhere in the gate gemms with 25 loads, and the run with 19 is no faster. **The slow clock** did not stay: the window from 816 is at 1.00 with waits of 0.31 and 0.49 in it. The pattern that the Trainium skill describes (TensorE: Matmul & The Clock Gate, "A second HAM failure mode: psum-queue depth-cycling") does not show at this size of pause. Behind waits of 2.52 and 4.16 the clock did fall, and behind one of 1.98 in one kernel of two.

The forecast landed within 1.5 us with errors of both signs: 1.1 from the gates, 0.9 from `w_ro` and 0.5 from head 0 against 1.2 in the tail and 0.7 at `w_o`. That they nearly cancel is luck.
